# Broadcasting one row of 512 floats: four identity matmuls and a copy, or a write to DRAM and a read onto all partitions

## The chip, the cores and the metric

The kernel runs on one core of a Trainium2 chip. The time is device microseconds of one execution of the whole block. Before the change the median of three runs is 731.25 us (730.97 to 731.89).

## What is computed

One layer of a residual block over 512 tokens (S) of width 1024 (D). With `rms_norm(x) = x / sqrt(mean(x*x) + 1e-6) * gain`:

```python
hn = rms_norm(x, norm1_g)
proj = hn @ w_in            # q_A k_A v_A | q_B k_B v_B | g_A g_B
out_a = chunked_attention(qa, ka, va, q_norm_g, k_norm_g, rel_bias)
out_b = stick_breaking_attention(qb, kb, vb)
mixed = sigmoid(g_A) * (out_a @ w_branch_a) + sigmoid(g_B) * (out_b @ w_branch_b)
x = x + mixed @ w_out
x = x + conv_glu(rms_norm(x, norm2_g), w_ffn_up, conv_w, conv_b, w_ffn_down)
```

Everything is float32. The kernel does not divide x by its rms before the first projection. It projects `x * gain` and multiplies the products by 1/rms of the token afterwards, where a product needs it.

## The kernel before

**Tiles and stages.** Tokens and features are cut into pieces of 128. A float32 product is made of three matmuls on rounded halves (`mm3`, lines 214 to 216, or line 334 for the first two chunks): high by high, high by low, low by high. Weights come in chunks of 128 x 2048 floats, in the order of the list `CHUNKS`: qA0, kA0, vA0, qA1, kA1, vA1, gA0, vB0 and so on. Each chunk is read from DRAM by SP's queue into `raw` (line 130, two buffers), cast by ACT into `whi` (line 188) and subtracted by DVE into `wlo` (line 190); for vA0 alone the subtraction is done by POOL. The stages are the first projections with attention A and then B between them (to about 310 us of the span), the output projection, the up projection with its convolution, and the down projection.

**What sets the order.** The program is written in one thread, and a scheduler of the framework sets the order of each engine's instructions from it, by its own estimate of times and by priorities (`tc.high_priority` on attention steps). Each engine, and SP's queue of transfers, then works strictly in that order: an instruction that waits holds up those behind it on its engine.

**The row of 1/rms.** `norm1(t)` (lines 296 to 304) sums the squares of 128 tokens on ACT (line 300), and POOL raises the mean to the power -0.5 (line 302). The result lies in `cols` as four columns: token t*128+p on partition p, column t (`rstd` is the first plane of `cols`). Where tokens lie along the free axis, the factor is needed as a row that stands on all partitions. `norm1_row()` (lines 306 to 313) makes it: for each t, a float32 matmul of the column, stretched to 128 equal columns, with the identity (line 309) puts 128 tokens of the row onto all partitions of a PSUM bank, and ACT copies the bank into the tile `rrow` (line 312). The function is called at line 680, after the first three attention steps are written. `rrow` is read by DVE at lines 469 (gates of A), 453 (k of B) and 499 (gates of B).

**Around it.** `a_stack` (line 418) transposes the normed q and k of attention A with the identity on PE (`qkT_A`, line 424); `stack_q` and `stack_k` (lines 403 to 416) cut them into halves on ACT and DVE; `qk_body` (line 371) makes the norm of q and k on ACT (line 378), DVE (lines 380, 382, 386) and POOL (line 385); `v_body` and `tok_groups` do the projection of v.

Of the kernel before, what the change touches and what calls it, by code (L numbers as in the profile page):

```python
# [8 lines left out]
F32 = mybir.dt.float32  # L9
# [6 lines left out]
P = 128  # L16
S = 512
D = 1024
NT = S // P
# [45 lines left out]
def block_kernel(ctx: ExitStack, tc: tile.TileContext, x, xt, params, g2, rbx, wts, wd0, wd1, out):  # L65
    nc = tc.nc
    V, A, G, PE, SP = nc.vector, nc.scalar, nc.gpsimd, nc.tensor, nc.sync
# [22 lines left out]
    ident = pool_c.tile([P, P], F32, tag="ident", name="ident")  # L90
# [133 lines left out]
    dram = ctx.enter_context(tc.tile_pool(name="dram", bufs=1, space=bass.MemoryType.DRAM))  # L224
# [7 lines left out]
    def ptile(tag, bufs, name):  # L232
        return pp.tile([P, S], F32, tag=tag, name=name, bufs=bufs)
# [3 lines left out]
    PV = lambda n: ptile("pv", 1, n)  # L237
# [21 lines left out]
    for i in range(WARM):  # L259
        PE.matmul(pw.rearrange("p (a b) -> p a b", a=4), warm, warm.unsqueeze(1).to_broadcast([P, 4, P]),  # L260
                  start=True, stop=True)
# [32 lines left out]
    rstd, nrstd, epsq = (cols[:, i, :] for i in range(3))  # L294
# [9 lines left out]
        V.tensor_scalar_mul(nrstd[:, c], rstd[:, c], -1.0)  # L304

    def norm1_row():
        ps = PV("rrow")
        for t in range(NT):
            PE.matmul(ps[:, t * P:(t + 1) * P], rstd[:, t:t + 1].to_broadcast([P, P]), ident,
                      start=True, stop=True)  # L310
        r = pool_c.tile([P, S], F32, tag="rrow", name="rrow")
        A.copy(r, ps)
        return r

    kg = par[:, C_KG:C_KG + 1]
# [362 lines left out]
    for s in range(LA):  # L678
        start_step(s)
    rrow = norm1_row()  # L680
    for s in range(len(steps)):
        if s + LA < len(steps):
# [5 lines left out]
        br, h, t, e = pend.pop(0)  # L688
# [412 lines left out]
```

## Time and profile before

| | |
|---|---|
| median of 3 runs | 731.25 us |
| the profiled execution | 730.74 us |
| its span in the profile | 729.0 us |
| PE (TensorE) busy | 723.3 us, 99% |
| DVE (VectorE) busy | 533.8 us, 73% |
| ACT (ScalarE) busy | 380.4 us, 52% |
| POOL (GpSimd) busy | 41.7 us, 6% |
| DMA packets of the 16 engines of q1, SP's queue | 32.5% of their span |
| granted TensorE clock | 0.999 |

The span runs from the first to the last instruction that the profiler saw; 1.74 us of the execution lie outside it. All times of rows are microseconds from the start of the span. PE is a matmul, PEld the loading of its weights, SPq the issuing of a transfer by SP. The kinds of views used are the page (busy times, the chain of work that ended last), waits by engine, the timeline of one engine in a window, windows with busy sums, tiles, and the list of DMA issues.

### The profile page before, as it was taken

What the parts mean: (1) busy time and instruction counts of PE and PEld (TensorE: products, weight loads), DVE (VectorE), ACT (ScalarE), POOL (GpSimd) and SP (SyncE); (2) the same over time, 40 slices, a digit from 0 to 9 for tenths busy, and PEclk for the clock granted to TensorE, in tenths of its full rate; (3) what the DMA queues carried; (4) which work ended last, traced back from release to release, by engine and by line L of the source; (5) the groups of instructions that cost most, each with busy time, mean ns of one, the idle gap of its engine ahead of it and who ended that gap; (6) DMA issues with size and microseconds to landing.
All of it is one profiled execution on the core that took longest, in us unless ns stands there. A gap on an engine that the chain in (4) does not pass through costs nothing.

```text
span 729.0 us, 10033 instructions
## 1 busy us (share of the span) xinstructions
PE 723.3 (99%) x3839; PEld 623.0 (85%) x3839; DVE 533.8 (73%) x967; ACT 380.4 (52%) x685; POOL 41.7 (6%) x73
## 2 busy tenths in 40 slices
PE   9999999999999999999999999999999999999997
PEld 8999998888988888888889888888888888888885
DVE  6678867775987888375275877667777675997686
ACT  6676556556856686343153553444554443543531
POOL 2701200000110111000000000000000000000000
PEclk9999999999999999999999999999999999999999
DMA  9632222121231112225342423223213313354563
GB/s 314 244 127 87 77 112 83 64 66 62 106 101 73 58 59 98 105 68 205 139 167 64 145 81 116 102 71 116 106 68 116 111 62 115 126 204 170 181 214 116
DMA packets 17905, 85.68 MB, mean 118 GB/s; under 512 B 2112, under 2 KB 2752, under 8 KB 10304
## 3 DMA queue, kind: packets, MB, share of 16 engines
q1 hardware_dynamic: 17568, 84.90, 32.5%
q8 instruction: 30, 0.49, 0.3%
q14 instruction: 19, 0.16, 0.1%
q10 hardware_dynamic: 288, 0.14, 0.1%
HBM read 80.84 MB, written 4.19 MB: 117 GB/s over the span
## 4 chain that ended last, share of the span: by engine, by line
PE 99%; DVE 0%; DVEq 0%; issue 0%
PE P L943 14%; PE pg L215 5%; PE pu L215 5%; PE pg L216 5%; PE pg L214 5%; PE pu L216 5%; PE pu L214 5%; PE qkB L216 2%; PE gB L216 2%; PE qkB L214 2%; PE gA L214 2%; PE gA L215 2%; PE gB L214 2%; PE gA L216 2%; PE qkB L215 2%; PE gB L215 2%
## 5 line engine op out<-in xcount | busy, mean ns | idle before, releaser
L190 DVE TENSOR_TENSOR wlo_up<-raw_up,whi_up 128x1024 fp32r<-128x1024 f32 (+1 forms) x50 | 52.4, 1093 | 47.1 <-ACT whi_up L188 47.1
L216 PE MATMUL pg<-hth,wlo_up 128*128 128x512 f32 (+1 forms) x192 | 71.2, 371 | 0.0
L215 PE MATMUL pu<-htl,whi_up 128*128 128x512 f32 (+1 forms) x192 | 71.2, 371 | 0.0
L214 PE MATMUL pg<-hth,whi_up 128*128 128x512 f32 (+1 forms) x192 | 71.2, 371 | 0.0
L214 PE MATMUL pu<-hth,whi_up 128*128 128x512 f32 (+1 forms) x192 | 71.2, 371 | 0.0
L215 PE MATMUL pg<-htl,whi_up 128*128 128x512 f32 (+1 forms) x192 | 71.1, 371 | 0.0
L216 PE MATMUL pu<-hth,wlo_up 128*128 128x512 f32 (+1 forms) x192 | 71.1, 370 | 0.0
L188 ACT CAST whi_up<-raw_up 128x1024 fp32r<-128x1024 f32 (+1 forms) x50 | 44.6, 948 | 27.2 <-PE pu L215 22.7
L943 PE MATMUL P<-whi_dn,ax 128*128 128x512 f32 x176 | 54.4, 389 | 0.0
L147 ACT CAST whi_dn<-raw_dn 128x1024 fp32r<-128x1024 f32 x33 | 34.3, 1052 | 27.9 <-PE P L943 19.9
L143 DVE TENSOR_TENSOR wlo_dn<-raw_dn,whi_dn 128x1024 fp32r<-128x1024 f32 x33 | 39.9, 1223 | 9.3 <-ACT whi_dn L147 9.3
L214 PEld LDWEIGHTS pu<-hth,whi_up 128*128 128x128 f32 x192 | 36.1, 188 | 6.3
L215 PEld LDWEIGHTS pg<-htl,whi_up 128*128 128x128 f32 x192 | 36.1, 188 | 6.2
L214 PEld LDWEIGHTS pg<-hth,whi_up 128*128 128x128 f32 x192 | 36.0, 188 | 6.3
L216 PEld LDWEIGHTS pg<-hth,wlo_up 128*128 128x128 f32 x192 | 36.1, 188 | 6.2
L216 PEld LDWEIGHTS pu<-hth,wlo_up 128*128 128x128 f32 x192 | 36.0, 188 | 6.2
L215 PEld LDWEIGHTS pu<-htl,whi_up 128*128 128x128 f32 x192 | 36.0, 188 | 6.2
L943 PE MATMUL P<-whi_dn,ay 128*128 128x512 f32 x132 | 40.8, 389 | 0.0
L943 PEld LDWEIGHTS P<-whi_dn,ax 128*128 128x128 f32 x176 | 33.0, 188 | 6.9
L806 ACT ACTIVATE cg<-pg,par 128x512 f32<-128x512 f32 x22 | 17.1, 778 | 39.4 <-PE pg L216 32.2
L943 PE MATMUL P<-wlo_dn,ax 128*128 128x512 f32 x88 | 34.2, 389 | 0.0
L588 DVE TENSOR_TENSOR_SCAN aB<-aB,reset 128x127 f32<-128x127 f32 (+3 forms) x32 | 26.0, 815 | 6.7 <-ACT aB L583 6.7
(250 smaller groups left out, 1970.2 us busy)
## 6 DMA issues: line engine op xcount, KB each, us to landing
raw_up<-in_wts SPq DMA_DIRECT2D x22, 1024.0 KB, 4.8
raw_dn<-in_wd SPq DMA_DIRECT2D x11, 1024.0 KB, 4.8
raw_dn<-in_wd SPq DMA_DIRECT2D x11, 512.0 KB, 3.3
raw_gA<-in_wts SPq DMA_DIRECT2D x4, 1024.0 KB, 4.8
raw_qkB<-in_wts SPq DMA_DIRECT2D x4, 1024.0 KB, 4.8
raw_gB<-in_wts SPq DMA_DIRECT2D x4, 1024.0 KB, 4.8
raw_wo<-in_wts SPq DMA_DIRECT2D x4, 1024.0 KB, 4.8
xs<-in_xt SPq DMA_DIRECT2D x8, 256.0 KB, 5.3
```

What stands on the lines that cost most here:

```text
L143: chain("halves", V.tensor_tensor(o, x, y, op=op))
L147: chain("casts", A.copy(hi[:, sl], src))
L188: A.copy(hi[:, sl], raw[:, sl])
L190: E.tensor_tensor(lo[:, sl], raw[:, sl], hi[:, sl].bitcast(F32), op=ALU.subtract)
L214: PE.matmul(ps, sh, mh, start=first, stop=False)
L215: PE.matmul(ps, sh, ml, start=False, stop=False)
L216: PE.matmul(ps, sl, mh, start=False, stop=last)
L588: V.tensor_tensor_scan(ar, ar, reset[:, S - n:S - 1][:, ::-1], 1.0, op0=ALU.mult, op1=ALU.max)
L806: tap = A.activation(c, ps, AF.Identity, scale=cw(2), bias=par[:, C_CB + tile_idx:C_CB + tile_idx + 1])
L943: chain("products", PE.matmul(dst, st, mv, start=first and n == 0, stop=last and n == 2, skip_group_check=True))
```

## The change

`norm1_row()` no longer uses PE, PSUM and ACT. SP writes the four columns of `rstd` to a DRAM tile of 4 x 128 floats, with the write's pattern turned so that the 512 floats lie in token order, and then reads those 512 floats onto each of the 128 partitions of `rrow` (a source step of 0 over the partitions). Nothing else in the source differs; lines below are numbered one less than before.

```diff
     def norm1_row():
-        ps = PV("rrow")
-        for t in range(NT):
-            PE.matmul(ps[:, t * P:(t + 1) * P], rstd[:, t:t + 1].to_broadcast([P, P]), ident,
-                      start=True, stop=True)
+
+        row = dram.tile([NT, P], F32, tag="row", name="row")
+        SP.dma_start(row.rearrange("t p -> p t"), rstd)
         r = pool_c.tile([P, S], F32, tag="rrow", name="rrow")
-        A.copy(r, ps)
+        SP.dma_start(r, bass.AP(row.tensor, row.offset, [[0, P], [1, S]]))
         return r
```

The scheduler orders all engines anew. Three places of that order follow.

PE, where the first projections end and vA0 begins; `qkT_A` are transposes, `rrow` the four matmuls. Before:

```order
L424 MATMUL qkT_A_510<-ident,n_qA_223 128x128 x2
L309 MATMUL rrow<-ident,cols 128x128 x4
L424 MATMUL qkT_A_510<-ident,n_qA_223 128x128 x2
L214 MATMUL vA_0_478<-whi_vA_377,hth 128x256
L214 MATMUL vA_1_636<-whi_vA_377,hth 128x256
L215 MATMUL vA_0_478<-wlo_vA_378,hth 128x256
```

The same place with the change:

```order
L423 MATMUL qkT_A_510<-ident,n_qA_223 128x128 x4
L214 MATMUL vA_0_478<-whi_vA_377,hth 128x256
L214 MATMUL vA_1_633<-whi_vA_377,hth 128x256
L215 MATMUL vA_0_478<-wlo_vA_378,hth 128x256
L216 MATMUL vA_0_478<-whi_vA_377,htl 128x256
```

The four matmuls are gone, and the projection of v follows the transposes at once.

SP's queue, from the bias tiles `tt` of the first two heads on; the `raw` tiles are weight chunks. Before:

```order
L541 DMA tt_669<-in_rbx 128x512
L130 DMA raw_vA_186<-in_wts 128x2048
L130 DMA raw_qA_348<-in_wts 128x2048
L130 DMA raw_kA_475<-in_wts 128x2048
L130 DMA raw_vA_713<-in_wts 128x2048
L130 DMA raw_gA_926<-in_wts 128x2048
```

The same place with the change:

```order
L540 DMA tt_666<-in_rbx 128x512
L130 DMA raw_vA_186<-in_wts 128x2048
L130 DMA raw_qA_348<-in_wts 128x2048
L309 DMA row<-cols 128x4x1
L311 DMA rrow<-row 128x512
L130 DMA raw_kA_475<-in_wts 128x2048
L130 DMA raw_vA_710<-in_wts 128x2048
L130 DMA raw_gA_923<-in_wts 128x2048
```

The write and the read-back stand between the weight chunks qA1 and kA1, so the load of kA1 is issued only after the read-back, which waits for the write to land.

DVE, where k is normed (`rs_kA`) and the stacked q of attention A (`sq_A`) and the low half of qA1 (`wlo_qA`) are made. Before:

```order
L380 TENSOR_REDUCE ss_kA_467<-sq_kA_465 128x8
L382 SCALAR_TENSOR_TENSOR rs_kA_461<-ss_kA_459,cols 128x8
L382 SCALAR_TENSOR_TENSOR rs_kA_469<-ss_kA_467,cols 128x8
L407 SCALAR_TENSOR_TENSOR sq_A_508<-qkT_A_510,qg_98,sq_A_508 64x512
L190 TENSOR_TENSOR wlo_qA_504<-raw_qA_348,whi_qA_503 128x512 x4
```

The same place with the change:

```order
L379 TENSOR_REDUCE ss_kA_467<-sq_kA_465 128x8
L381 SCALAR_TENSOR_TENSOR rs_kA_461<-ss_kA_459,cols 128x8
L406 SCALAR_TENSOR_TENSOR sq_A_508<-qkT_A_510,qg_98,sq_A_508 64x512
L381 SCALAR_TENSOR_TENSOR rs_kA_469<-ss_kA_467,cols 128x8
L190 TENSOR_TENSOR wlo_qA_504<-raw_qA_348,whi_qA_503 128x512 x4
```

Two neighbours changed places; the split of qA1 still comes behind both.

## Rows read from the trace of the kernel before

**Rows 1.** The page: busy time, share of the span, instructions of each engine.

```profile
PE 723.3 (99%) x3839; PEld 623.0 (85%) x3839; DVE 533.8 (73%) x967; ACT 380.4 (52%) x685; POOL 41.7 (6%) x73
```

**Rows 2.** Waits of PE, whole span: us in total, times, longest.

```profile
PE warm L260 <- DVE warm L257: 1.1, 1, 1.1
```

**Rows 3.** Chain that ended last: start us, us, what.

```profile
28.38 0.89 PE rrow L309 x8
...
38.33 0.66 PE qkT_A L424 x6
44.91 0.44 PE qkT_A L424 x4
...
724.43 0.42 DVE x L948
```

**Rows 4.** Windows, 28 to 310 us: us, busy (x) by engine, clock, DMA, GB/s.

```profile
28.00:310.00 282.00, 282.00 (x1703) 250.51 (x1702) 218.02 (x501) 179.72 (x395) 28.54 (x47) 1.00 0.25 87
```

**Rows 5.** Timeline of PE: start us, us, what [idle before <-releaser].

```profile
29.57 0.28 PE L215 MATMUL vA<-wlo_vA,hth 128*128 128x256 f32 x1
29.68 0.28 PE L216 MATMUL vA<-whi_vA,htl 128*128 128x256 f32 x1
...
51.13 0.27 PE L606 MATMUL pT_A<-ident,eA 128*128 128x128 f32 x1
```

**Rows 6.** Timeline of POOL, 23 to 32 us.

```profile
23.77 0.55 POOL L302 TENSOR_TENSOR cols<-ss,nhalf 128x1 f32<-128x1 f32 x1 [0.18 <-DVE cols L304]
...
26.46 5.07 POOL L190 TENSOR_TENSOR wlo_vA<-raw_vA,whi_vA 128x512 fp32r<-128x512 f32 x4 [0.52 <-ACT whi_vA L188]
```

**Rows 7.** Timeline of ACT, 27 to 48 us.

```profile
27.96 1.09 ACT L378 ACTIVATE sq_kA<-kA 128x512 f32<-128x512 f32 x2
29.31 0.59 ACT L312 COPY rrow<-rrow 128x512 f32<-128x512 f32 x1 [0.26 <-PE rrow L309]
29.79 0.68 ACT L406 ACTIVATE sq_A<-qkT_A,qg 64x512 fp32r<-64x512 f32 x1
...
43.11 2.17 ACT L188 CAST whi_kA<-raw_kA 128x512 fp32r<-128x512 f32 x4
...
47.08 0.40 ACT L562 ACTIVATE eA<-sA,st 128x128 f32<-128x128 f32 x1
```

**Rows 8.** Timeline of DVE, 30 to 49 us.

```profile
31.59 0.74 DVE L407 SCALAR_TENSOR_TENSOR sq_A<-qkT_A,qg,sq_A 64x512 fp32r<-64x512 f32 x1
32.36 0.69 DVE L190 TENSOR_TENSOR wlo_qA<-raw_qA,whi_qA 128x512 fp32r<-128x512 f32 x1
...
48.25 0.55 DVE L565 TENSOR_SCALAR eA<-eA,st 128x128 f32<-128x128 f32 x2
```

**Rows 9.** Timeline of SP's queue, 16 to 35 us.

```profile
16.81 0.33 SPq L130 DMA_DIRECT2D raw_qA<-in_wts  x1
31.56 0.33 SPq L130 DMA_DIRECT2D raw_kA<-in_wts  x1
```

**Rows 10.** DMA issues: what, queue, count, KB each, median us to landing.

```profile
tt<-in_rbx SPq DMA_DIRECT2D x8, 256.0 KB, 3.3
...
out<-x SPq DMA_DIRECT2D x7, 256.0 KB, 2.1
...
raw_qA<-in_wts SPq DMA_DIRECT2D x1, 1024.0 KB, 11.3
raw_kA<-in_wts SPq DMA_DIRECT2D x1, 1024.0 KB, 4.8
...
par<-in_params ACTq DMA_DIRECT2D x1, 4.0 KB, 2.8
```

**Rows 11.** Tile rrow: xcount, ns min/median/max, first and last start us.

```profile
L469 DVE TENSOR_TENSOR mixA<-gA,rrow x8: 668/688/692, 91.9 to 184.2; 128x512 f32<-128x512 f32 x8
```

**Rows 12.** Tile whi_gA, a matmul of 512 columns: ns min/median/max.

```profile
L214 PE MATMUL gA<-hth,whi_gA x64: 387/389/478, 85.7 to 182.4; 128*128 128x512 f32 x64
```

**Rows 13.** Groups by line and form, 28 to 310 us: xcount, busy us, mean ns.

```profile
L214 PE MATMUL gA<-hth,whi_gA 128*128 128x512 f32 x64 | 25.3, 396 | 0.0
```

## The prediction

> **What bounds the kernel now.** I read the page first, for who is busy: PE 723.3 us of a span of 729.0, DVE 73%, ACT 52% [rows 1]. Then the waits of PE: in the whole span it waited once, 1.1 us before its first matmul [rows 2]. The chain of work that ended last agrees, being PE from the first microseconds to 724.43 us, where DVE's last addition begins [rows 3]. In the window in which anything can move, 28 to 310 us, PE is busy 282.00 of 282.00 us [rows 4]. So the time is the sum of what PE is given. Work of other engines and of the queues counts only if it makes PE wait, and work taken from PE counts in full unless PE runs into a wait instead. The row to look at is the one of the four matmuls: they stand on the chain at 28.38 us, as eight records (two to each float32 matmul), with 0.89 us [rows 3].
>
> **What is removed.**
>
> PE: four matmuls, 0.89 us [rows 3]. They were not hidden, since PE waits for nothing there. Term: **-0.89 us**.
>
> ACT: the copy of the bank, 0.59 us from 29.31 us [rows 7]. ACT is not the bound. Its next work, the first half of the stacked q, can follow the squares of k, which end at 27.96 + 1.09 = 29.05 us, and so starts at 29.05 instead of 29.79 us [rows 7]. Term: 0.
>
> **What is added.** Two transfers on SP's queue.
>
> The write waits for POOL's last power, which ends at 23.77 + 0.55 = 24.32 us [rows 6]. SP's last issue before it was at 16.81 and its next is at 31.56 us [rows 9], so SP stands free and issues the write at about 24.4. How long it takes is not in the trace: it moves 512 separate floats, and no transfer there is cut so small. I bound it by rows. The least is an output write on idle DMA engines, 2.1 us, landing at 26.5. The most is four times the one transfer with small pieces, the 4 KB of `par` in 128 pieces, 2.8 us [rows 10], begun only when the chunk in front of it (qA1) has landed at 16.81 + 11.3 = 28.1 [rows 9, 10]: 28.1 + 11.2 = 39.3. I take 28.1 + 2.8 = 30.9, by the nearest row in size and pieces, behind the same chunk. Then the read-back is issued (0.33 us) and lands after 3.3 us, the time of a bias tile of the same 256 KB, at about 34.5. The first reader of the row is DVE at 91.9 us [rows 11]: 57 us to spare, and 49 us even at the far end. Term: 0.
>
> Behind the read-back in SP's queue stands the load of kA1, issued at 31.56 us before. With the write landing at 30.9 it is issued at 31.56 as before, waiting for the same buffer. At the far end it is issued at 39.3 + 0.33 = 39.6 and lands 4.8 us later, at 44.4, where ACT wants it at 43.11 [rows 7]: ACT stands 1.3 us. The exponentials behind it in ACT's queue begin at 47.08, DVE is done with the first two at 48.25 + 0.55 = 48.80 [rows 8], and PE takes them at 51.13 [rows 5], so 2.3 us of cover are left and PE loses nothing even there. Term: 0, at both ends.
>
> [...]
>
> **What moves.** PE comes 0.89 us earlier to work that others prepare, so I ask what is late next.
>
> First, the low half of vA0 from POOL. POOL makes its four pieces from 26.46 to 31.53 us [rows 6], 1.27 us each, and nothing there moves. PE took the first at 29.57, with 0.118 us to a matmul (29.57 and 29.68, and so on) [rows 5]. With the change it is there at 28.68, when the first piece has been ready since 27.73; the second is wanted 12 matmuls later, at 30.1, and ready at 29.0; the third after 13 more at 31.6, ready at 30.3. No wait, with about 1 us left.
>
> Then the low half of qA1 from DVE, which the new order wants earlier than the old one: after 12 more matmuls, at 33.0. Before, DVE had its first piece at 32.36 + 0.69 = 33.05 [rows 8]. The change lets DVE come to it sooner, since `sq_A`, in front of it at 31.59, now goes ahead of its neighbour, and ACT's part of it comes 0.7 us sooner. At most 0.05 us are lost. Term: 0.
>
> Further on, to about 300 us, the scheduler has swapped many neighbours on PE. I counted how often its order changes between transposes and other matmuls: 132 times before, 146 with the change, so seven more groups of transposes. On the chain a group of six takes 0.66 us and one of four 0.44 [rows 3]: 0.110 us for each transpose either way, so nothing for the group that these rows can show. They are rounded to 0.01 us; with twice that for each, seven groups are 0.14 us. Term 0, bound +0.14.
>
> **The sum.** 730.74 (the profiled execution) - 0.89 = 729.85 us. That execution lies 0.51 us under the median of the runs, 731.25. For the median I therefore forecast 731.25 - 0.89 = 730.36, that is **730.4 us**, 0.12% less. A measurement of this kernel can tell about 0.2% (1.46 us) from no change, so this forecast counts as no change.
>
> **The rivals.**
>
> *The gain is given back.* PE meets new waits in the rewritten order between 50 and 300 us, where others' results come a little before PE takes them. For it: DVE works 218 of 282 us there [rows 4], and a place such as the first transposes of attention has 2.3 us of cover (above), no more. Against it: the old order, made by the same scheduler, has no wait at all in 282 us. With 0.89 us of waits the time is 731.25; with three such places it is 730.36 + 2.7 = 733.1.
>
> *SP's queue is held up, and the kernel is slower.* Place: the load of kA1 behind the read-back. It may be issued 43.11 - (31.56 + 4.8) = 6.75 us late before ACT sees it, and 2.3 us more before PE does. So the point from which it decides is a write that lands at 31.56 + 9.05 - 0.33 = 40.3, some 16 us after its issue; each us beyond costs one. To be slower than 731.25 by over 0.2% it must land after 42.6. If the 512 pieces cost twice my far end, it lands at 28.1 + 22.4 = 50.5 and the kernel takes 730.4 + 10.2 = 740.6 us. For it: no row bounds a piece of four bytes from above with certainty. Against it: no other transfer is under way from 28.1 to 31.56 us [rows 9, 10], and even four times `par` stays below the point. [...]
>
> *More is gained than the four matmuls.* A matmul of 512 columns has a median of 389 ns [rows 12] and a mean of 396 [rows 13]; nine groups of some 64 in this window look so, which makes up to 9 x 64 x 7 ns = 4 us of lengthened matmuls. If the new order, with ACT free 0.6 us sooner, avoids a quarter of these, the time is 730.4 - 1.0 = 729.4; with half, 728.4. Against it: most of that length is the change from one shape to another, and the new order has more such changes.
>
> That the change does not take place is no rival: the four matmuls are gone from PE's order.
>
> **How the numbers follow.** Forecast, 0.66: its own range is 729.9 to 730.9, from the 0.14 and the scatter of the runs about their median, and 0.04 of it may be read as faster. Given back, 0.19: 0.16 as no change, 0.03 as slower. Queue held up, 0.06: slower. More gained, 0.09: faster. So faster 0.13, same 0.78, slower 0.09. The range 729.2 to 732.4 takes in the forecast, most of the first rival and half of the third; it leaves out the second and the tails, some 0.15.
>
> **What would show it.** Right: PE's busy time lower by 0.9 us, no wait of PE after its start, vA0 beginning near 28.4 us, the write landing before 40 and kA1 issued near 31.6. Wrong: a wait of PE between 28 and 310 us; a landing of the write over 16 us after its issue; kA1 issued after 40 us; or PE without waits and yet shorter by clearly more than 0.9 us.

## The result, and the profile after

The changed kernel takes 733.28 us (median of 9 runs, 731.85 to 733.97) where the kernel before, on the same chip, took 731.31 (9 runs, 730.67 to 731.89): a ratio of 1.0025, with a 95% interval of 1.0015 to 1.0035. It is slower by about 2 us, where 0.9 less was forecast. The profiled execution took 732.88 us, with a span of 731.2.

PE has less to do, and yet the end comes later. The busy line of the page, against [rows 1]:

```profile
PE 722.6 (99%) x3831; PEld 621.5 (85%) x3831; DVE 533.3 (73%) x967; ACT 379.2 (52%) x684; POOL 41.3 (6%) x73
```

Eight matmul records and 0.7 us are gone from PE. The waits of PE (us in total, times, longest), against the single one of [rows 2]:

```profile
PE qA L214 <- ACT whi_qA L188: 1.8, 1, 1.8
PE warm L260 <- DVE warm L257: 1.1, 1, 1.1
PE qA L333 <- ACT whi_qA L188: 0.7, 1, 0.7
PE s_A L549 <- DVE st L557: 0.3, 1, 0.3
```

The first is new: PE stands 1.8 us for the high half of qA1, which ACT casts. The third lies at the start, before 28 us, and comes in most of the later profiles, one of them with the old order, so it is not the change's. The windows (columns as in [rows 4]) agree:

```profile
28.00:310.00 282.00, 279.78 (x1687) 248.00 (x1686) 217.66 (x501) 178.66 (x394) 28.05 (x47) 1.00 0.25 88
```

Of 282 us PE now misses 2.22. With the 0.89 us of the matmuls and the 0.71 us of the start (26.18 us busy before 28 us, 26.89 in the profile of before) that makes -0.89 + 2.22 + 0.71 = +2.04, and the span is 2.2 us longer. The chain between 16 and 36 us (start, us, what) tells what ACT itself waited for:

```profile
16.96 15.93 DMA raw_qA<-in_wts
32.97 0.63 ACT whi_qA L188
...
33.64 0.39 PE qA L214
```

The load of qA1 was issued at 16.96 us and landed 15.93 later. The DMA issues, against [rows 10] (KB each, us to landing), and SP's timeline, against [rows 9]:

```profile
raw_qA<-in_wts SPq DMA_DIRECT2D x1, 1024.0 KB, 15.9
raw_kA<-in_wts SPq DMA_DIRECT2D x1, 1024.0 KB, 7.6
...
rrow<-row SPq DMA_DIRECT2D x1, 256.0 KB, 5.6
...
row<-cols SPq DMA_DIRECT2D x1, 2.0 KB, 8.5
```

```profile
16.96 0.33 SPq L130 DMA_DIRECT2D raw_qA<-in_wts  x1
24.57 0.39 SPq L309 DMA_DIRECT2D row<-cols  x1
33.07 0.33 SPq L311 DMA_DIRECT2D rrow<-row  x1
```

The same load took 11.3 us before [rows 10]. It now lands at 16.96 + 15.93 = 32.89, hardly 0.2 us ahead of the write that was issued 7.6 us behind it and landed at 33.07. The DMA engines were not busy meanwhile; the last columns of the windows are their share and GB/s:

```profile
26.00:27.00 1.00, 1.00 (x11) 1.00 (x11) 0.69 (x1) 1.00 (x3) 0.80 (x2) 1.00 0.64 149
27.00:28.00 1.00, 1.00 (x12) 1.00 (x11) 0.00 (x0) 0.84 (x2) 1.00 (x2) 1.00 0.06 17
28.00:29.00 1.00, 1.00 (x11) 1.00 (x10) 0.19 (x1) 0.82 (x2) 1.00 (x2) 1.00 0.21 16
29.00:33.00 4.00, 2.87 (x25) 2.67 (x23) 2.42 (x5) 0.85 (x3) 4.00 (x3) 1.00 0.00 0
```

Nearly all of the load's data has moved by 27 us and the last of it by 28, but its landing is told 5 us later, as is the write's. The semaphore events of the trace show this more closely. In both traces the landing of this load shows as 16 increments of a semaphore. Before, they came between 26.24 and 28.16 us. Now ten come by 28.63 us and the other six one after another until 32.89, while those of the write, on another semaphore, run from 26.85 to 33.05.

### The profile page after: what moved, and what is told of

It is laid out like the page before. It is cut to its first block, busy times and chain, and to the rows that moved or that the text cites. A ratio compares the mean times of both kernels' runs of the same rounds, so it can differ in the third digit from the quotient of the medians.

```text
span 731.2 us, 10025 instructions
## 1 busy us (share of the span) xinstructions
PE 722.6 (99%) x3831; PEld 621.5 (85%) x3831; DVE 533.3 (73%) x967; ACT 379.2 (52%) x684; POOL 41.3 (6%) x73
## 2 busy tenths in 40 slices
DMA packets 18577, 85.95 MB, mean 118 GB/s; under 512 B 2656, under 2 KB 3296, under 8 KB 10976
## 4 chain that ended last, share of the span: by engine, by line
PE 94%; DMA 4%; DVE 0%; ACT 0%; SPq 0%; issue 0%; DVEq 0%; ACTq 0%
PE P L942 14%; PE pg L214 5%; PE pu L214 5%; PE pg L215 5%; PE pu L215 5%; PE pg L216 5%; PE pu L216 5%; DMA raw_qA<-in_wts 2%; PE qkB L215 2%; PE gB L216 2%; PE gB L214 2%; PE qkB L214 2%; PE qkB L216 2%; PE gB L215 2%; PE wo L215 2%; PE wo L216 2%
```

## The experiments

17 experiments ran, one of them the changed kernel again, each beside the kernel before on the same chip. Unless said otherwise, diffs are against the changed kernel, and each engine's order is the changed kernel's but for what the diff adds. The first theory, A in the expectations, was: the early write holds back the landing of qA1's chunk, and the new order makes PE wait for it.

**The write behind kA1's load.** The new order stays; the write goes elsewhere (`behind` sets the order on SP's queue).

```diff
+    loads = {}
...
-            SP.dma_start(raw[:, sl], wts[i, :, sl])
+            loads[order[i]] = SP.dma_start(raw[:, sl], wts[i, :, sl])
...
-        SP.dma_start(row.rearrange("t p -> p t"), rstd)
+        behind(SP.dma_start(row.rearrange("t p -> p t"), rstd), (loads["kA1"],))
```

> The write of the row is put behind the load of kA1 in SP's queue; the order of PE, DVE, ACT and POOL is that of the changed kernel, row for row. In the changed kernel the chunk qA1 took 15.9 us to land (11.3 before) beside the write, and PE waited 1.8 us for its cast. Theory A (the early write holds up the landing of qA1): qA1 lands in about 11.3 us again, PE has no wait at qA1, and the time falls by 1.8 us from 733.3 to about 731.5, or to 730.4 to 730.8 if the waits of 0.3 and 0.7 us in the changed kernel's profile go as well. kA1 now lands late, some 40 us, still before ACT takes it at 43 us. Theory B (the rewritten order of the engines is what costs): the order is unchanged, so the time stays at 733.3 us, with PE waiting as long as before. Theory C (the hold-up of kA1 in SP's queue costs): kA1's landing barely moves, so the time stays at 733.3.

730.99 us (730.51 to 731.79), ratio 0.9997 (0.9989 to 1.0006). The load of qA1 lands after 11.7 us and PE does not wait for it. The write, now in the midst of the loads of kA1 and vA1, takes 12.8 us, and nobody feels it. So the new order alone is not slow.

**The old order with the early write.** Against the kernel before: matmuls and copy stay, the write and a read-back that nobody reads are added.

```diff
         A.copy(r, ps)
+        row = dram.tile([NT, P], F32, tag="row", name="row")
+        SP.dma_start(row.rearrange("t p -> p t"), rstd)
+        r2 = pool_c.tile([P, S], F32, tag="rrow2", name="rrow2")
+        SP.dma_start(r2, bass.AP(row.tensor, row.offset, [[0, P], [1, S]]))
```

> The kernel before, with its four matmuls and the copy, and beside them the early write and a read-back into a tile that nobody reads; the order of PE, DVE, ACT and POOL is that of the kernel before, row for row. Theory A: the chunk qA1 lands in about 16 us as in the changed kernel, its cast ends near 33.6 us; PE in the old order comes to qA1 first at 33.8, so PE waits 0 to 0.3 us there and the time is 731.3 to 731.6. Then the price of the write depends on the order it meets. Theory B (order alone): the old order gives 731.3, and qA1 lands at about 11.3 us. A price of the transfers wherever they stand: 733 us.

730.98 us, ratio 0.9997 (0.9988 to 1.0007). The load is held back as in the changed kernel, 15.6 us, and ACT waits for it (its timeline):

```profile
32.74 2.18 ACT L188 CAST whi_qA<-raw_qA 128x512 fp32r<-128x512 f32 x4 [1.60 <-DMA raw_qA<-in_wts]
```

PE is busy 282.00 of 282.00 us all the same: the old order takes qA1's first matmul behind 38 matmuls of vA0 and the four of the row, the new one behind 26 of vA0. In this run PE comes to it at 34.47 us, when the first piece is some 1.1 us old. So neither part of the change is slow by itself; the price comes from the late landing and the earlier demand together.

**The write on ACT's queue.**

```diff
-        SP.dma_start(row.rearrange("t p -> p t"), rstd)
+        A.dma_start(row.rearrange("t p -> p t"), rstd)
```

> The early write is issued by ACT, into ACT's own queue, at about the same time, 24.5 us; the rest is the changed kernel's. If qA1 is held up because the 512 small pieces stand behind it in one queue, qA1 lands in 11.3 us, PE has no wait at qA1, and the time is about 731.5 (or 730.8). If the hold-up comes from the DMA engines, whichever queue feeds them, qA1 takes some 16 us as before and the time stays at 733.3. Issuing costs ACT some 0.4 us where it is idle anyway.

732.39 us, ratio 1.0018 (1.0009 to 1.0027); the load lands after 15.6 us, the write after 8.6, and PE waits 1.5 us. So SP's queue is not what ties the two, and this run does not show what does.

**Other sizes of piece.** 128 pieces of 16 bytes (the row permuted in DRAM, so that tokens change their factors), and 256 of 8 bytes (likewise).

```diff
-        SP.dma_start(row.rearrange("t p -> p t"), rstd)
+        SP.dma_start(row.rearrange("t p -> (t p)").rearrange("(p t) -> p t", t=NT), rstd)
```

> The write goes in 128 pieces of 16 bytes in place of 512 of 4, at the same time and place. The row then lies in DRAM in another order (token t*128+p at place 4p+t), so the factors that are read back belong to other tokens; the work of all engines is the changed kernel's. If the hold-up goes with the number of pieces, a quarter of the 4.6 us is left: qA1 lands in about 12.4 us, the write in about 4 us, PE has no wait at qA1 and the time is about 731.5. If any write at this place costs it, qA1 stays at 16 us and the time at 733.3.

731.20 us, ratio 1.0000 (0.9991 to 1.0009): the load 12.0 us, the write 4.3, no wait for qA1.

```diff
-        SP.dma_start(row.rearrange("t p -> p t"), rstd)
+        SP.dma_start(row.rearrange("t p -> (t p)").rearrange("(a p b) -> p a b", a=2, b=2), rstd.rearrange("p (a b) -> p a b", a=2))
```

> The write goes in 256 pieces of 8 bytes, same place and time. The row then lies in DRAM in another order, so the factors that are read back belong to other tokens; the work of all engines is the changed kernel's. With 128 pieces qA1 landed in 12.0 us and the write in 4.3; with 512 in 15.6 to 15.9 and 8.3 to 8.6. If the price goes with the number of pieces, 256 give 13.2 us for qA1 and 5.7 us for the write; the cast then starts by 30.4 us, PE has no wait at qA1, and the time is 731.2. If it goes with the bytes or with pieces under 16 bytes, it is as with 512: 733.3.

730.97 us, ratio 1.0000 (0.9990 to 1.0009): the load 12.2, the write 4.7, no wait.

**Four rows of 512 bytes**, by a transpose on PE and a small copy on ACT.

```diff
-        SP.dma_start(row.rearrange("t p -> p t"), rstd)
+        ps = PV("rrow")
+        PE.transpose(ps[0:NT, 0:P], rstd, ident)
+        r4 = pool_c.tile([NT, P], F32, tag="r4", name="r4")
+        A.copy(r4, ps[0:NT, 0:P])
+        SP.dma_start(row, r4)
```

> One transpose of the four columns on PE (0.11 us in place of 0.89) and a copy on ACT turn them into four rows of 512 bytes; the write then goes in 4 pieces. It is issued about 29.5 us, since it waits for PE and ACT. The order of the engines is that of the changed kernel but for this one transpose. Theory A (the number of small pieces holds up completions): write 2 to 3 us, qA1 lands in 11.3 to 12 us, no wait of PE at qA1, and the time is that of the run with the write behind kA1 plus the transpose: about 731.1. The 0.46 us of waits near 122 us, which came with the new order, should be there again. Rival (any write to DRAM from this place holds PE up): about 733.

730.95 us, ratio 1.0000 (0.9991 to 1.0008). The write is issued at 30.07, after qA1's landing (11.2 us), and the read-back follows at 31.27. So this run is no test of the hold; it shows again that the new order is not slow without it.

**The write with nothing beside it.** It waits on POOL for kA1's landing, and vA1's load waits for the read-back.

```diff
...
+            if order[i] == "vA1":
+                behind(loads["vA1"], late["row"])
...
-        SP.dma_start(row.rearrange("t p -> p t"), rstd)
+        rc = pool_c.tile([P, NT], F32, tag="rc", name="rc")
+        G.tensor_copy(rc, raws[pos["kA1"]][:, 0:NT])
+        G.tensor_copy(rc, rstd)
+        behind(SP.dma_start(row.rearrange("t p -> p t"), rc), (loads["kA1"],))
...
-        SP.dma_start(r, bass.AP(row.tensor, row.offset, [[0, P], [1, S]]))
+        late["row"] = (SP.dma_start(r, bass.AP(row.tensor, row.offset, [[0, P], [1, S]])),)
```

> The write of 512 pieces waits until kA1 has landed (POOL first copies four floats of kA1 into the source tile, then the factors over them), and the load of vA1 stands behind the read-back, so the write has the DMA engines to itself. If the 512 pieces need the time by themselves, it lands in about 8 us as in the changed kernel (8.5). If it was slow because a chunk was under way, it lands in about 3 us, as the 4 KB of parameters did. Either way qA1 lands in about 11.5 us, PE has no wait at qA1, and the time is about 731.0, as with the write behind kA1; the load of vA1 lands near 50 us, before ACT takes it at 55.6.

730.66 us, ratio 0.9993 (0.9983 to 1.0003). With no other load under way the write still takes 10.4 us:

```profile
row<-rc SPq DMA_DIRECT2D x1, 2.0 KB, 10.4
```

So it is slow by itself, not by the traffic beside it.

**The write twice**, to two rows.

```diff
+        row2 = dram.tile([NT, P], F32, tag="row2", name="row2")
+        SP.dma_start(row2.rearrange("t p -> p t"), rstd)
```

> The early write is made twice, the second time into a DRAM tile that nobody reads: 1024 pieces of 4 bytes instead of 512, same order of PE, DVE, ACT and POOL as the changed kernel. Theory A: the landing of qA1 is held up by both, 15.9 + 4 to 5 = 20 to 21 us, the cast starts near 37.5 us, PE waits some 6 us there instead of 1.8, and the time rises by 4 to 5 us to 737 to 738. Rivals (order, or SP's queue): no change from 733.3 beyond 0.4 us.

732.16 us, ratio 1.0013 (1.0004 to 1.0023): a miss. The load lands after 15.9 us, as with one write, and both writes after 8.8. The hold does not grow with the number of pieces in flight. Nor does it come in every execution: four of the ten runs, at 730.59 to 731.53 us, look as if nothing had been held; they were not profiled.

**A second, unread write of 512 four-byte pieces, behind the row in 16-byte pieces (permuted as above).** Packed into 2 KB, 64 bytes apart, and 512 bytes apart (`w` of 16 and 128):

```diff
-        SP.dma_start(row.rearrange("t p -> p t"), rstd)
+        SP.dma_start(row.rearrange("t p -> (t p)").rearrange("(p t) -> p t", t=NT), rstd)
+        far = dram.tile([NT, P], F32, tag="far", name="far")
+        SP.dma_start(far.rearrange("t p -> p t"), rstd)
```

```diff
+        far = dram.tile([S, w], F32, tag="far", name="far")
+        SP.dma_start(far.rearrange("(t p) w -> p t w", t=NT)[:, :, 0], rstd)
```

> The row itself is written in 128 pieces of 16 bytes, and right behind it the same 512 values go once more to a second DRAM tile of 2 KB in 512 pieces of 4 bytes, as in the changed kernel. No program part reads the second tile. Both theories expect the price to be back, since 512 packed 4-byte pieces are in flight beside qA1's chunk: raw_qA lands after 15 to 16 us (12.0 with the 16-byte pieces alone), PE waits 1.3 to 1.8 us at qA, time 732.0 to 733.3. If neither is right (the read-back behind the write, or the row's own tile, made the price), raw_qA lands after 12 us and the time is 731.0 to 731.3.

> As the run with the second write packed, but its 512 pieces of 4 bytes go to places 64 bytes apart in a DRAM tile of 32 KB. Theory M (the pieces are slow because many of them fall into the same short stretch of DRAM and are taken one after the other there; two writes to two rows ran side by side and cost no more than one): raw_qA lands after 11.5 to 12.5 us, PE does not wait at qA, time 731.0 to 731.3. Theory N (the number of 4-byte pieces in one transfer decides, wherever they go): raw_qA 15 to 16 us, PE waits 1.3 to 1.8 us, time 732.0 to 733.3.

> As before with 512 bytes between the pieces, in a DRAM tile of 256 KB. Theory M, also where the stretch that serialises is longer than 64 bytes: raw_qA after 11.5 to 12.5 us, no wait of PE at qA, time 731.0 to 731.3. Theory N: raw_qA 15 to 16 us, PE waits 1.3 to 1.8 us, 732.0 to 733.3. If the 64-byte step is slow and this one is not, M holds with a stretch between the two.

730.57, 730.37 and 730.57 us; ratios 0.9994 (0.9985 to 1.0003), 0.9990 (0.9981 to 0.9999) and 0.9993 (0.9984 to 1.0002). The issues of the first and of the second:

```profile
raw_qA<-in_wts SPq DMA_DIRECT2D x1, 1024.0 KB, 11.7
...
row<-cols SPq DMA_DIRECT2D x1, 2.0 KB, 4.1
far<-cols SPq DMA_DIRECT2D x1, 2.0 KB, 7.2
```

```profile
row<-cols SPq DMA_DIRECT2D x1, 2.0 KB, 4.1
far<-cols SPq DMA_DIRECT2D x1, 2.0 KB, 3.9
```

Two things follow. The same number of four-byte pieces takes 7.2 us when they are packed side by side and 3.9 when they lie 64 bytes apart (3.8 at 512): what makes this write slow is that its pieces fall next to one another in DRAM (theory M), and not their number (theory N). And the packed control missed in both theories: a write of 7.2 us was in flight beside qA1's chunk and held nothing back. A slow write is not enough.

**What decides.** Two theories were left: the moment at which the packed pieces come (T), or that they stand directly behind the load (F). First a transfer of 16 bytes ahead of the write, then the packed write first with the 16-byte pieces behind it, and the changed kernel again:

```diff
+        far = dram.tile([NT, P], F32, tag="far", name="far")
+        SP.dma_start(far[0:1, 0:NT], rstd[0:1, :])
         SP.dma_start(row.rearrange("t p -> p t"), rstd)
```

> The changed kernel with one transfer of 16 bytes from a single partition issued on SP just ahead of the packed write, so that the packed write is issued about 0.4 us later (25.0 to 25.3 us, 24.57 to 24.82 before) and is otherwise the same. Theory T (the moment decides: pieces that come while the last pieces of qA1's chunk are still queued hold back its landing, later ones do not): raw_qA lands after 11.5 to 12.5 us, PE does not wait at qA, median 730.4 to 731.2. Theory F (being first behind the load on a DMA engine decides; 15 of 16 engines see no difference): raw_qA 15 to 16 us, PE waits 1.3 to 1.8 us, median 732.0 to 733.3.

> The unread packed write of 512 4-byte pieces first, at 24.6 to 24.9 us, and the row in 128 pieces of 16 bytes behind it. Theories T and F both: raw_qA lands after 15 to 16 us, PE waits 1.3 to 1.8 us, median 732.0 to 733.3. If raw_qA lands after 12 us here too, the second, packed write is not what holds, and what decided in the changed kernel is that the row itself, which the read-back waits for, was the packed one.

> The changed kernel, unchanged, beside the same runs of the kernel before. All theories: median 732.7 to 733.6, ratio 1.0020 to 1.0035, raw_qA 15 to 16 us in the profile. Theory T expects that some runs escape (under 731.7, as with the write doubled, where 4 of 10 did), since the last pieces of the load are near the point of issue; theory F expects all above 731.8.

With the tiny transfer: 731.22 us, ratio 0.9996 (0.9988 to 1.0005), the load 11.8 us, no wait for it, although the write behind took 8.0. Packed first: 732.37 us (5 runs), ratio 1.0027 (1.0011 to 1.0044), the load 15.5, a wait of 1.4. The changed kernel: 732.68 us (732.01 to 737.47), ratio 1.0022 (1.0011 to 1.0034), the load 15.9, a wait of 1.7; none of its 12 runs escaped. It issued its write 8.01 us after the load (17.04 and 25.05), the kernel with the tiny transfer 8.25 (16.81 and 25.06). Measured by what was expected of them, the tiny transfer came out as T says and F does not, and the 12 runs as F says and T does not. (That 15 of 16 engines see no difference with the tiny transfer was my assumption; no run shows it.) F in a wider form (any transfer between, however small, frees the load: F2) fits both, but for T a threshold between 8.01 and 8.25 was not excluded. The last two separate them: the packed write later and still first (four copies on DVE, which is idle there), and at its old moment with a transfer ahead, made from a value that is ready sooner.

```diff
+        rc = rstd
+        for i in range(4):
+            rn = pool_c.tile([P, NT], F32, tag=f"rc{i}", name=f"rc{i}")
+            V.tensor_copy(rn, rc)
+            rc = rn
-        SP.dma_start(row.rearrange("t p -> p t"), rstd)
+        SP.dma_start(row.rearrange("t p -> p t"), rc)
```

> The changed kernel, with the column of 1/rms passed through four small copies on DVE (which is idle from 24.7 to 26.2 us in the changed kernel's trace) before the same packed write: it is first behind the load on the queue, but issued 8.3 to 8.7 us after the load's issue, where 7.5 to 8.0 us held the landing back. Theory T (the moment decides): raw_qA lands after 11.5 to 12.5 us, PE does not wait at qA for it, median 730.5 to 731.4. Theory F2 (what decides is that no other transfer stands between load and packed write): raw_qA 15 to 16.5 us, PE waits 1.3 to 2.3 us, median 732.0 to 733.5.

```diff
+        sss.append(ss)
...
+        far = dram.tile([1, NT], F32, tag="far", name="far")
+        SP.dma_start(far[0:1, 0:1], sss[-1][0:1, :])
         SP.dma_start(row.rearrange("t p -> p t"), rstd)
```

> A 4-byte transfer of a value that is ready about 0.6 us before the column goes ahead on the queue, so that the packed write keeps its moment (7.5 to 7.9 us after the load's issue) but is not first behind the load. Theory T: raw_qA 15 to 16 us, PE waits 1.3 to 1.8 us, median 732.0 to 733.3. Theory F2: raw_qA 11.5 to 12.5 us, no wait, median 730.5 to 731.4.

Later: 737.22 us (737.07 to 737.97, 4 runs), ratio 1.0085 (1.0070 to 1.0100); the load is held, as F2 expected, but the time lies above its 732.0 to 733.5, for a reason told in the last section. With the neighbour: 730.51 us, ratio 0.9993 (0.9983 to 1.0003). SP's timeline and the load's time of the one, then of the other:

```profile
17.28 0.33 SPq L130 DMA_DIRECT2D raw_qA<-in_wts  x1
25.99 0.39 SPq L314 DMA_DIRECT2D row<-rc  x1
34.81 0.34 SPq L316 DMA_DIRECT2D rrow<-row  x1
```

```profile
raw_qA<-in_wts SPq DMA_DIRECT2D x1, 1024.0 KB, 17.4
```

```profile
16.99 0.33 SPq L130 DMA_DIRECT2D raw_qA<-in_wts  x1
23.90 0.30 SPq L313 DMA_DIRECT2D far<-ss  x1
24.52 0.39 SPq L314 DMA_DIRECT2D row<-cols  x1
32.22 0.34 SPq L316 DMA_DIRECT2D rrow<-row  x1
```

```profile
raw_qA<-in_wts SPq DMA_DIRECT2D x1, 1024.0 KB, 11.5
```

The moment is out: 8.7 us after the load the write still holds it, and 7.5 us after it does not if four bytes stand between. Counted from the end of the load's data it is out as well, as far as the views of the DMA engines show it, in slices of 0.45 us: in the changed kernel the last slice in which the load's data moves begins at 27.25 us, 2.7 us after the write's issue, and with 16 bytes ahead, where nothing was held, at 27.70, 2.6 us after it.

In each of the seven profiles in which the packed write stood directly behind the load of qA1 (one of them with the write on ACT's queue), the load landed late and within 0.7 us of the write: 32.89 and 33.07 in the changed kernel, 34.63 and 34.81 here. In the five with larger pieces directly behind it, the two also landed close together (28.92 and 29.11 with 16 bytes). But a load with nothing behind it landed at 27.9 to 29.0 us, so these five show no hold. This fits the two misses: with two writes the load landed with them and no later, and in the control the write directly behind was the quick one.

**The late write in 16-byte pieces**, tried as the version to keep: the first experiment's place with the third's pieces (its row is permuted too).

> The version that the runs point to: four matmuls gone, the write in 128 pieces of 16 bytes and issued behind kA1's load, so that nothing small is in flight beside qA1's chunk. Both theories: raw_qA 11 to 12 us, no wait at qA, PE busy 722.6 (0.7 less than before), but 0.3 to 0.5 us of it given back near 122 us where gA waits for DVE, so 730.6 to 731.1, a ratio to the kernel before of 0.9990 to 1.0000; a median under 730.4 would say that the give-back is not there.

730.91 us, ratio 0.9997 (0.9988 to 1.0006). It is no worse than before and not measurably better. Of all versions only the one with pieces 64 bytes apart has an interval that ends under 1, at 0.9999, and it carries a useless write, so no version is claimed to beat the kernel before. Taken together, the eleven versions of the new order in which PE did not wait for qA1 lie between 0.08 above and 0.69 us below the runs of before beside them, 0.3 below on average.

## Why the prediction was wrong

By its own steps:

- **Four matmuls, -0.89 us: right, but not all of it kept.** Where nothing else disturbs, in the version with the early tiny transfer, PE is busy 26.89 us of the first 28, just as before, and the windows show what is left over:

```profile
28.00:310.00 282.00, 281.54 (x1695) 249.62 (x1695) 217.81 (x501) 178.68 (x395) 28.68 (x47) 1.00 0.26 88
120.00:125.00 5.00, 4.54 (x23) 3.43 (x22) 4.79 (x18) 4.72 (x16) 0.00 (x0) 1.00 0.46 180
```

  All of the 0.46 us that PE misses falls into 120 to 125 us, where it stands for the statistics of DVE (`PE s_A L554 <- DVE st L562`, 0.3 us) and a little more. -0.89 + 0.46 = -0.43, and that span is 728.5 against 729.0. So the rival "more is gained than the four matmuls" did not come. What I held against it is in the trace of before: between 28 and 310 us a matmul of 512 columns takes 447 ns behind one of another shape (median of 75) and 389 behind one of its own (658). The rival "the gain is given back" had the right kind of place, for half of the gain, and in the old order the same stretch had no idle time. Its conditional times (731.25 and more) were not reached by this alone.
- **The write's own landing: in its bounds.** I took 30.9 from the 4 KB of `par` and gave 26.5 to 39.3; it landed at 33.07, 8.5 us after its issue. That it came only 2.2 us after my guess is partly luck. I gave the write 2.8 us from the landing of the chunk ahead. It takes 8.5 us here, and 10.4 with no other load under way, since its pieces lie side by side in DRAM (7.2 us against 3.9 at 64 bytes apart); but it did not wait for that landing, and its first increment came at 26.85 us, before it.
- **What stands behind it in SP's queue: right.** kA1's load was issued at 33.51 instead of 31.56, ACT cast it at 44.98 instead of 43.11, and PE did not wait. The rival "SP's queue is held up" asked for a landing after 40.3 and did not decide.
- **"Term: 0" for the write: this step failed.** I looked for harm only behind the write, at kA1 and at the row's reader. In the same step I used qA1's landing at 28.1 as a fixed number from which to start the write, although that chunk was still under way when the write was issued. It is the chunk ahead that was held, from 28.1 to 32.89.
- **"What moves": this step left out what made it cost.** I followed the low halves of vA0 and qA1 into the new order and granted at most 0.05 us for qA1, but I did not ask for its high half, whose first matmul the new order takes 12 matmuls of vA0 earlier, besides the four that are gone. PE's timeline has it before, in the changed kernel, and in the version with one transfer of 16 bytes ahead, where the landing is on time:

```profile
33.80 0.28 PE L214 MATMUL qA<-whi_qA,hth 128*128 128x256 f32 x1
```

```profile
33.64 0.39 PE L214 MATMUL qA<-whi_qA,hth 128*128 128x256 f32 x1 [1.77 <-ACT whi_qA L188]
```

```profile
31.44 0.28 PE L214 MATMUL qA<-whi_qA,hth 128*128 128x256 f32 x1
```

  So the new order wants it at 31.44 us, and with the landing held PE cannot have it before 33.64. The old order asked for it at 33.80, and so hid the same lateness. The range ended at 732.4 without this case: of the two that reached beyond it, one was three new waits between 50 and 300 us (733.1), the other a hold-up at another transfer.

I took the write for a transfer of many small pieces, and priced it at the wrong transfer. The page shows the pieces: packets under 512 bytes rise from 2112 to 2656, by the 512 pieces and the 32 increments of the two new transfers. The count is not the price, though, since the same 512 pieces take 3.9 us when they lie 64 bytes apart and 7.2 packed. The hold does not go with the queue either: the write on ACT's queue held the load as long (15.6 us). Why a write that is issued 7.6 us later holds back the landing of a load whose data has moved, and why four bytes between them undo it, no run shows. **This stays open**: the runs show when the hold occurs and what it costs, not what makes it.

Two more facts bear on it. The load is not the only transfer that is late: by the trace's DMA packets, a 16 KB packet of the queue that the page calls `q8 instruction`, begun at 28.91 us, took 3.3 us in the changed kernel, and the one begun at 28.89 us took 0.9 before. And with another load the picture differs. In the first experiment the write stood directly behind kA1's chunk, 0.4 us after it and with vA1's chunk behind. There kA1 landed after 8.0 us, 5 us ahead of the write; with the 16-byte pieces in the same place it landed after 6.0. The loads of vA0 and vA1 have a median of 11.5 us in the one and 7.7 in the other.

## What to carry to other kernels

When a change adds a transfer, ask what it does to the transfers that are still under way when it is issued, not only to what is queued behind it; a landing read from the old trace is no constant (qA1 took 11.3 us before and 15.9 after). A write like this one, 512 single words side by side in DRAM (8.5 us), should be cut into larger pieces (4.3 us in pieces of 16 bytes), or be put where no load that is needed soon stands directly ahead of it (with the write behind kA1's load, qA1's landed after 11.7 us). And when an edit rewrites the order, list every tile that the bounding engine now takes earlier, and compare it with the landing, not only with the engine that prepares it.

## What the runs showed of the hardware

- **Words side by side were slow.** 512 pieces of 4 bytes land after 7.2 to 10.4 us packed (10.4 with idle DMA engines) and 12.8 between two loads, after 3.9 when 64 bytes apart; 256 pieces of 8 bytes take 4.7 and 128 of 16 bytes 3.9 to 4.3 (5.8 between two loads).
- **A load landed with the write behind it.** In the changed kernel 1 MB whose data had moved by 28 us was told as landed at 32.89 us, 0.2 us ahead of the packed write directly behind it. In the seven profiles with this arrangement the load took 15.5 to 17.4 us, against 11.2 to 11.8 with nothing behind it; one transfer of 4 or 16 bytes between the two undid it (11.5 and 11.8).
- **A wait of 3.2 us came with half the clock.** With the packed write later, PE stood 3.23 us, from 32.15 to 35.38, and while it stood its granted clock fell from 1.00 to 0.50, by the windows at 34.6 us. That the wait brought it about is my reading of this profile alone. The windows of that kernel (the clock is the third column from the end):

```profile
33.00:34.00 1.00, 0.00 (x0) 0.00 (x0) 0.00 (x0) 0.00 (x0) 1.00 (x1) 1.00 0.00 0
34.00:34.70 0.70, 0.00 (x0) 0.00 (x0) 0.00 (x0) 0.00 (x0) 0.70 (x2) 0.93 0.00 0
...
36.00:37.00 1.00, 1.00 (x6) 1.00 (x6) 1.00 (x3) 0.97 (x3) 0.00 (x0) 0.50 0.78 35
...
41.50:42.00 0.50, 0.50 (x7) 0.50 (x6) 0.00 (x0) 0.00 (x0) 0.00 (x0) 1.00 0.93 393
```

  It stayed there until 41.4 us (0.57 in the window from 41.0 to 41.5): PE worked some 6 us of that at half speed, which by estimate (6 us at 0.50) loses about 3 more, and the kernel took 6.2 us more than before. After the wait of 1.8 us of the changed kernel the clock stayed at 1.00. Two of the 12 runs of the changed kernel's repetition, at 734.61 and 737.47 us, have a mean granted clock of 0.996 and 0.995 where the others have 0.999 or 1.000, which looks like the same thing; they were not profiled.
